# Running the second half of a projection chunk's blocks one piece of weights behind the first half

## The chip, the cores and the metric

The kernel runs on one core of one Trainium2 chip. Its time is the device time of one execution in microseconds, and the number compared is the median over several executions. Engines are named as in the profile: PE is TensorE, with PEld for its weight loads, DVE is VectorE, ACT is ScalarE, POOL is GpSimd, and SP is the queue that issues the DMAs.

## What is computed

The reference is a decoder trunk of two layers over 256 tokens of width 2048, all in float32. Cut to what matters here, one layer is:

```python
h = rms_norm(x, pre_g)
p = split_columns(h @ w_in + b_in)        # 2048 x 6992: 14 groups of up to 512 columns here
o_sb  = stick_breaking_attention(...)     # four head groups, each reads its columns of p
o_nsa = native_sparse_attention(...)      # compressed keys and values by two small networks
o_fox = forgetting_attention(...)
o_mla = latent_attention(...)             # low-rank: w_uq and w_ukv on 512 columns of p
mix = concatenate([o_g * silu(gate_g) for g in (sb, nsa, fox, mla)])
x = x + rms_norm(mix @ w_out, post_g)
```

Most of the work is `h @ w_in`, with `mix @ w_out` next. The change touches the order of the first.

## The kernel before, in words

**Operands.** The normalised input stands transposed in eight tiles `hcat`, one for each pair of K tiles of 128 rows. Each holds a high part of all 256 tokens and beside it the low part (what rounding to the high part left). The weights come as a stream of *pieces* (class `Stream`, L170): a piece is 256 rows by up to 512 columns, loaded into a `raw` tile by DMA, and split by two instructions for each of its two halves: ACT copies `raw` into the high part `whi` (`hi()`, L211), then DVE subtracts that from `raw` into the low part `wlo` (`lo()`, L226). A product is the sum of high by high, high by low and low by high.

**Chunks.** A *chunk* is one group of columns against all of K, so eight pieces. `chunk()` (L573) works on two to four *blocks*, each with an accumulator of one PSUM bank. A T block (`mm_t()`, L640) gives 128 output columns as partitions: for each half of a piece one matmul of 512 columns (high weights against both parts of `hcat`, L648) and one of 256 (low weights, L649). Its two sums are added on evacuation (`evac_t()`, L664: ACT copies one half, DVE adds, POOL multiplies by the norm factor). A K block (`mm_k()`, L652) has 128 tokens as partitions: six matmuls for a piece (L660), and DVE evacuates it (`k_out()`, L632). `t_group()` (L672) is a chunk of four T blocks, `k_group()` (L721) one of two K blocks, and `nsa_kv()` (L1056) has two T blocks and one with both token halves. The accumulators come from a pool of four banks that are taken in turn, `mm`.

In `chunk()` the loop over pieces is the outer one, and every piece goes through all the blocks before the next:

```python
for ks in range(NK // 2):
    hi, lo = self.ws.get()
    for i, (b, o) in enumerate(zip(blocks, acc)):
        ...                       # the block's matmuls with this piece
        if last:
            evac(i, o)
    self.ws.free()
```

`first_chunk()` (L594) and `out_proj()` (L1412) have loops of their own.

**Order.** The order on every engine is written out by the program itself; engines wait for each other by semaphores. A planner keeps an estimated clock of PE and of the queues on DVE, ACT and POOL. After every few matmuls `pump()` (L287) moves PE's clock on and lets one step of one waiting task (attention heads, gates, rotations, the compression networks) write its instructions when the estimates say that its inputs are there, so that those matmuls and transposes stand between the projection's. Then `Stream.tick()` (L239) may write one split. `get()` (L252) writes whatever of the next piece isn't split yet. Splits run ahead of use up to a limit that counts from the last *freed* piece: eight `whi`/`wlo` tiles, of which `spare` (two) stay back. `raw` loads follow the splits, up to four pieces (L207), and other loads are put between them on SP (`later()`, L358).

**The places spoken of below.** In each layer `nsa_q()` (L1155), a chunk of two K blocks, is followed by `mla_up()` (L939). That takes one piece of `mla_w_ukv` and three of `mla_w_uq` (384 columns a half), and its matmuls are on L955: the products for v (evacuated by ACT to `mv`), for kn (DVE copies to `kn`), for qr and for qn. Each matmul for qr reads both halves of a piece (`heads()`, L968). Then come the mla gate, a K chunk of 336 columns, `nsa_kv()`, the nsa gate, the sb queries, keys and values, and so on. `qq` is the rotated nsa query that PE transposes on L1176; `pc` (L1250) is the softmax of the compressed branch; `w` are the weights of the compression networks (L1115), loaded in four parts for keys and four for values.

Of the kernel before, what the change touches and what calls it, by code (L numbers as in the profile page):

```python
# [19 lines left out]
S = 256  # L20
# [3 lines left out]
NK = D // P  # L24
# [243 lines left out]
class Kernel:  # L268
# [304 lines left out]
    def chunk(self, blocks, evac):  # L573

        acc = self.accs(len(blocks))
        for ks in range(NK // 2):
            last = ks == NK // 2 - 1
            hi, lo = self.ws.get()  # L580
            for i, (b, o) in enumerate(zip(blocks, acc)):
                if b[0] == "T":
                    self.mm_t(o, hi, lo, b[1], ks)
                elif b[0] == "K":
                    self.mm_k(o[:, :b[3]], self.h_at(ks, b[1]), hi, lo, b[2], b[3], ks == 0, last)
                else:
                    for t in range(2):
                        self.mm_k(o[:, t * S:(t + 1) * S], self.h_at(ks, t), hi, lo, b[1], S, ks == 0 and t == 0, last)
                if last:
                    self.now()  # L590
                    evac(i, o)
            self.ws.free()

    def first_chunk(self, l, cols):  # L594

# [996 lines left out]
```

## Time and profile before

| | |
|---|---|
| median of 3 runs | 949.1 us (948.77 to 949.96) |
| the profiled execution | 947.95 us |
| its span, first to last instruction | 946.2 us |
| PE, PEld busy | 924.5, 782.6 us |
| DVE, ACT, POOL busy | 604.9, 521.8, 119.0 us |
| matmuls of the T blocks (L648, L649) | 396.2 + 304.0 us busy |
| matmuls of the K blocks (L660 on `hcat`) | 229.9 + 138.9 us busy |
| TensorE clock granted, mean | 0.998 |

A line of a timeline reads: start, duration, engine, source line, operation, out<-in, shapes, count, and in brackets the idle time before it with what ended it. A line of the waits reads: who waited for whom, us in total, times, longest. Matmuls overlap in the pipeline, so two rows' starts tell the pace, and their durations do not add up. Most instructions of DVE, ACT and POOL have the line of one recording helper (L127), so they are told apart by their tiles.

### The profile page before, as it was taken

The numbers are of one execution on the slowest core, as the hardware profiler recorded it, in microseconds if no ns is written. First come the engines' busy times: TensorE is split into PE (matmuls) and PEld (weight loads), VectorE is DVE, ScalarE is ACT, GpSimd is POOL, SyncE is SP. The second block draws the span as 40 slices with busy tenths as digits, with TensorE's granted clock in tenths as the row PEclk, the third lists the DMA queues.
The fourth block names the chain that finished last, engine by engine and source line by source line (L and its number), as shares of the span: only waits on it lengthen the run. The fifth ranks groups of instructions, "written<-read, shape, count | busy, mean of one in ns | idle before, by whom it ended". The sixth has DMA issues, their size and how long they took to land.

```text
span 946.2 us, 14525 instructions
## 1 busy us (share of the span) xinstructions
PE 924.5 (98%) x5186; PEld 782.6 (83%) x5186; DVE 604.9 (64%) x1324; ACT 521.8 (55%) x1176; POOL 119.0 (13%) x190
## 2 busy tenths in 40 slices
PE   7999999999999999999999999999999999999996
PEld 6888988877888888888878999878778888888885
DVE  6786777646666656754486867676457675557552
ACT  6745554544567554744476565456355775447540
POOL 0231011111011210100002210212100221001000
PEclk9999999999999999999999999999999999999999
DMA  7857656784354754579368575478644455646852
GB/s 269 271 180 192 188 180 184 238 252 120 115 155 132 225 189 127 162 265 307 96 200 269 161 191 182 137 212 260 200 122 136 154 152 184 209 134 220 263 185 89
DMA packets 116912, 177.65 MB, mean 188 GB/s; under 512 B 15860, under 2 KB 39400, under 8 KB 116840
## 3 DMA queue, kind: packets, MB, share of 16 engines
q1 hardware_dynamic: 116840, 176.73, 60.5%
q8 instruction: 40, 0.66, 0.3%
q14 instruction: 32, 0.26, 0.1%
HBM read 172.51 MB, written 4.19 MB: 187 GB/s over the span
## 4 chain that ended last, share of the span: by engine, by line
PE 88%; DMA 6%; DVE 3%; ACT 2%; POOL 1%; issue 1%; SPq 0%; POOLq 0%; DVEq 0%; ACTq 0%
PE mm L660 39%; PE mm L648 24%; PE mm L649 12%; PE sp L761 3%; DMA raw<-w_in 2%; PE mm L955 2%; PE op L805 1%; DMA w<-nsa_cmp_w_k 1%; DMA w<-nsa_cmp_w_v 1%; PE sp L793 1%; PE op L1115 1%; PE op L806 1%; ACT whi L127 1%; PE sp L496 1%; DVE wlo L127 1%
## 5 line engine op out<-in xcount | busy, mean ns | idle before, releaser
L127 DVE TENSOR_TENSOR wlo<-raw,whi 128x512 fp32r<-128x512 f32 (+2 forms) x592 | 389.3, 702 | 68.3 <-ACT whi L127 67.3
L648 PE MATMUL mm<-hcat,whi 128*128 128x512 f32 x1088 | 396.2, 405 | 2.3 <-DVE cmpT L127 1.2
L127 ACT ACTIVATE whi<-raw 128x512 fp32r<-128x512 f32 (+2 forms) x592 | 331.1, 613 | 117.1 <-DMA raw<-w_in 69.7
L649 PE MATMUL mm<-hcat,wlo 128*128 128x256 f32 x1088 | 304.0, 279 | 0.0
L648 PEld LDWEIGHTS mm<-hcat,whi 128*128 128x128 f32 x1088 | 204.5, 188 | 52.6 <-issue 4.5
L660 PE MATMUL mm<-whi,hcat 128*128 128x512 f32 (+2 forms) x768 | 229.9, 371 | 0.8 <-DVE tgrp L127 0.8
L649 PEld LDWEIGHTS mm<-hcat,wlo 128*128 128x128 f32 x1088 | 205.4, 189 | 0.2
L660 PEld LDWEIGHTS mm<-whi,hcat 128*128 128x128 f32 x768 | 139.1, 189 | 22.1 <-DVE tgrp L127 2.0
L660 PE MATMUL mm<-wlo,hcat 128*128 128x512 f32 (+2 forms) x384 | 138.9, 362 | 1.3 <-DVE wlo L127 1.3
L660 PE MATMUL mm<-whi,mxh 128*128 128x512 f32 x256 | 99.8, 390 | 0.0
L660 PE MATMUL mm<-whi,mxl 128*128 128x512 f32 x256 | 99.6, 389 | 0.0
L660 PE MATMUL mm<-wlo,mxh 128*128 128x512 f32 x256 | 99.6, 389 | 0.0
L127 POOL TENSOR_TENSOR tgrp<-tgrp,rr 128x256 f32<-128x256 f32 x64 | 58.3, 933 | 255.2 <-DVE tgrp L127 255.0
L660 PEld LDWEIGHTS mm<-wlo,hcat 128*128 128x128 f32 x384 | 72.6, 189 | 11.6 <-DVE wlo L127 2.9
L660 PEld LDWEIGHTS mm<-whi,mxl 128*128 128x128 f32 x256 | 48.0, 188 | 10.0
L660 PEld LDWEIGHTS mm<-whi,mxh 128*128 128x128 f32 x256 | 48.1, 188 | 10.0
L660 PEld LDWEIGHTS mm<-wlo,mxh 128*128 128x128 f32 x256 | 48.1, 188 | 9.9
L127 ACT ACTIVATE z<-z,nm 128x128 f32<-128x128 f32 x64 | 28.5, 447 | 48.2 <-DVE nm L127 47.1
L127 DVE TENSOR_TENSOR tgrp<-mm,tpart 128x256 f32<-128x256 f32 x64 | 26.1, 420 | 45.0 <-ACT tpart L127 44.8
L127 DVE CUSTOM_DVE_ANT_0 z<-sp,cst 128x128 f32<-128x128 f32 x64 | 20.3, 355 | 40.5 <-PE sp L761 40.4
L127 ACT ACTIVATE tpart<-mm 128x256 f32<-128x256 f32 x68 | 24.6, 380 | 37.8 <-PE mm L649 37.6
L127 DVE TENSOR_TENSOR y<-mm,bct 128x512 f32<-128x512 f32 x16 | 11.1, 692 | 51.3 <-ACT junk L127 51.3
(223 smaller groups left out, 755.1 us busy)
## 6 DMA issues: line engine op xcount, KB each, us to landing
raw<-w_in SPq DMA_DIRECT2D x207, 512.0 KB, 4.5
raw<-w_out SPq DMA_DIRECT2D x64, 512.0 KB, 5.0
x<-x SPq DMA_DIRECT2D x24, 256.0 KB, 6.3
raw<-w_in SPq DMA_DIRECT2D x16, 268.0 KB, 3.6
w<-nsa_cmp_w_k SPq DMA_DIRECT2D x8, 512.0 KB
w<-nsa_cmp_w_v SPq DMA_DIRECT2D x8, 512.0 KB, 6.2
raw<-mla_w_uq SPq DMA_DIRECT2D x6, 384.0 KB, 5.0
bct<-b_in SPq DMA_DIRECT2D x8, 256.0 KB, 5.3
```

The lines of the kernel that those rows point to most:

```text
L127: return f(out, *args, **kw)
L496: nc.tensor.transpose(ps[:, k * P:(k + 1) * P], x[:, k * P:(k + 1) * P], self.ident)
L648: nc.tensor.matmul(o, wh, h, start=(ks + kk == 0), stop=False, skip_group_check=True)
L649: nc.tensor.matmul(o[:, :S], wl, h[:, :S], start=False, stop=last, skip_group_check=True)
L660: nc.tensor.matmul(o, x, w, start=(first and kk == 0 and i == 0), stop=(last and kk == 1 and i == 2), skip_group_check=True)
L761: nc.tensor.matmul(sp[:, a:a + s1], q[:, q0:q0 + P], k[:, :s1], start=(i == 0 and a == 0), stop=(i == n - 1), skip_group_check=True)
L793: nc.tensor.transpose(sp[:, i * P:(i + 1) * P], z[:, i * P:(i + 1) * P], self.ident)
L805: nc.tensor.matmul(o, v0, pt[:, :256], start=start, stop=False, skip_group_check=True)
L806: nc.tensor.matmul(o[:, 128:256], v1, pt[:, 256:384], start=False, stop=stop, skip_group_check=True)
L955: nc.tensor.matmul(o, a, b, start=(i == 0 and o is first[0]), stop=(i == len(mms) - 1), skip_group_check=True)
L1115: nc.tensor.matmul(hp[g:g + 32, :P], blks[i][:, q * 8 + j, :], ws[q][:, j * P:(j + 1) * P], start=(q == 0 and j < 4), stop=(q == 3 and j > ...
```

## The change

Within `chunk()` the blocks are divided into an early half (`len(blocks) // 2`) and a late half. Step by step the early blocks take piece `step`, and then the late blocks take piece `step - 1`. A piece is freed after the late blocks have used it, so two pieces are held while the early blocks run. The chunk has nine steps instead of eight: in the first only the early blocks run, in the last only the late ones. The early blocks' accumulators are evacuated at the end of their last piece, when the late blocks still have two pieces to go. No matmul, split or load is added or removed. Since the planner writes side work and splits between the matmuls, their places move as well.

```diff
         acc = self.accs(len(blocks))
-        for ks in range(NK // 2):
-            last = ks == NK // 2 - 1
-            hi, lo = self.ws.get()
-            for i, (b, o) in enumerate(zip(blocks, acc)):
...
-                if last:
-                    self.now()
-                    evac(i, o)
-            self.ws.free()
+        n = NK // 2
+        held = {}
+
+        def run(i, ks):
+            b, o = blocks[i], acc[i]
+            hi, lo = held[ks]
+            last = ks == n - 1
...
+            if last:
+                self.now()
+                evac(i, o)
+
+        early = len(blocks) // 2
+        for step in range(n + 1):
+            if step < n:
+                held[step] = self.ws.get()
+                for i in range(early):
+                    run(i, step)
+            if step:
+                for i in range(early, len(blocks)):
+                    run(i, step - 1)
+                self.ws.free()
```

The lines left out hold the three kinds of block, which are the same on both sides. In the changed kernel everything below `chunk()` stands 14 lines lower: L648, L649, L660 and L955 there are L662, L663, L674 and L969.

More of the change, by code (lines that the diff above doesn't have):

```diff
@@ L577, in chunk @@
         acc = self.accs(len(blocks))
-        for ks in range(NK // 2):
-            last = ks == NK // 2 - 1
-            hi, lo = self.ws.get()
-            for i, (b, o) in enumerate(zip(blocks, acc)):
[L582 to L588, printed above, removed]
-                if last:
-                    self.now()
-                    evac(i, o)
-            self.ws.free()
+        n = NK // 2
[4 more added lines that the diff above has]
+            last = ks == n - 1
+            if b[0] == "T":
+                self.mm_t(o, hi, lo, b[1], ks)
+            elif b[0] == "K":
+                self.mm_k(o[:, :b[3]], self.h_at(ks, b[1]), hi, lo, b[2], b[3], ks == 0, last)
+            else:
+                for t in range(2):
+                    self.mm_k(o[:, t * S:(t + 1) * S], self.h_at(ks, t), hi, lo, b[1], S, ks == 0 and t == 0, last)
+            if last:
[11 more added lines that the diff above has]
+                self.ws.free()
     def first_chunk(self, l, cols):
```

## The prediction

> **What bounds the kernel now.** I read the page first, then the list of waits, then the timelines of the places that the list names.
>
> ```profile
> PE 924.5 (98%) x5186; PEld 782.6 (83%) x5186; DVE 604.9 (64%) x1324; ACT 521.8 (55%) x1176; POOL 119.0 (13%) x190
> PEclk9999999999999999999999999999999999999999
> PE 88%; DMA 6%; DVE 3%; ACT 2%; POOL 1%; issue 1%; SPq 0%; POOLq 0%; DVEq 0%; ACTq 0%
> ```
>
> TensorE is busy for 924.5 of 946.2 us at a clock that is full in every slice, and 88% of the chain that ended last is PE. The matmuls themselves are the same before and after, so the change can only act on what is left: the time in which PE waits, some 22 us with the start and the end. PE's own waits, longest first, from the list of waits filtered to PE:
>
> ```profile
> PE sp L496 <- DMA x<-x: 3.1, 2, 2.0
> PE op L460 <- DMA grow<-pre_norm_g: 2.5, 1, 2.5
> PE mm L660 <- DVE wlo L127: 1.3, 1, 1.3
> PE op L1115 <- DMA w<-nsa_cmp_w_v: 1.3, 2, 0.9
> PE mm L648 <- DVE cmpT L127: 1.2, 2, 0.7
> PE mm L648 <- DVE tgrp L127: 1.1, 2, 0.6
> PE op L1115 <- DMA w<-nsa_cmp_w_k: 1.1, 1, 1.1
> PE sp L1250 <- POOL pc L127: 0.9, 2, 0.5
> PE mm L660 <- DVE tgrp L127: 0.8, 1, 0.8
> PE sp L1176 <- DVE qq L127: 0.5, 1, 0.5
> ```
>
> Only the three rows on cmpT and tgrp belong to chunk() itself: 1.2 + 1.1 + 0.8 = 3.1 us in five waits. They are the first matmuls of a chunk that wait until the accumulator of the chunk before has been evacuated. One of them, from the chunk of the sb queries to that of the sb keys in layer 0 (timeline of all engines, start and duration in us):
>
> ```profile
> 189.61 0.28 PE L649 MATMUL mm<-hcat,wlo 128*128 128x256 f32 x1
> 189.94 0.91 ACT L127 ACTIVATE tpart<-mm 128x256 f32<-128x256 f32 x3
> 189.97 0.28 PE L649 MATMUL mm<-hcat,wlo 128*128 128x256 f32 x1
> 190.33 0.76 DVE L127 TENSOR_TENSOR tgrp<-mm,tpart 128x256 f32<-128x256 f32 x2 [1.45 <-ACT tpart L127]
> 190.81 0.50 PE L648 MATMUL mm<-hcat,whi 128*128 128x512 f32 x1 [0.57 <-DVE tgrp L127]
> 191.15 0.28 PE L649 MATMUL mm<-hcat,wlo 128*128 128x256 f32 x1
> 191.27 0.40 PE L648 MATMUL mm<-hcat,whi 128*128 128x512 f32 x1
> ```
>
> In steady flow an L649 start is followed by the next L648 start after 0.12 us (191.15 to 191.27); here it takes 0.84 us (189.97 to 190.81). So a wait costs 0.72 us where the list says 0.57: the pipeline runs empty as well. Five such waits cost 3.1 + 5 x 0.15 = 3.9 us.
>
> **The change part by part.** *The end of a chunk.* On TensorE, at this same boundary, the first matmul of each block in the rows before (hcat_274 is the last pair of K tiles; mm_1976 to mm_1979 are the four accumulators of the queries, mm_2292 and mm_2293 the first two of the keys, which take the banks of the queries' first two):
>
> ```order
> L648 MATMUL mm_1977<-hcat_274,whi_2074 128x512
> ...
> L648 MATMUL mm_1978<-hcat_274,whi_2074 128x512
> ...
> L648 MATMUL mm_1979<-hcat_274,whi_2074 128x512
> ...
> L648 MATMUL mm_2292<-hcat_135,whi_2124 128x512
> ...
> L648 MATMUL mm_2293<-hcat_135,whi_2124 128x512
> ```
>
> The same place now, where mm_2010 to mm_2013 are the queries' and mm_2292 and on the keys':
>
> ```order
> L662 MATMUL mm_2011<-hcat_274,whi_2104 128x512
> ...
> L662 MATMUL mm_2012<-hcat_273,whi_2093 128x512
> ...
> L662 MATMUL mm_2013<-hcat_273,whi_2093 128x512
> ...
> L662 MATMUL mm_2012<-hcat_274,whi_2104 128x512
> ...
> L662 MATMUL mm_2013<-hcat_274,whi_2104 128x512
> ...
> L662 MATMUL mm_2292<-hcat_135,whi_2144 128x512
> ...
> L662 MATMUL mm_2293<-hcat_135,whi_2144 128x512
> ```
>
> Between an accumulator's last matmul and the first one that overwrites its bank three blocks stood, and now five stand. A T block is two pairs of L648 and L649, and a pair takes 0.35 us (189.61 to 189.97 in the rows above), so a block takes 0.7 and the cover grows from 2.1 to 3.5 us. At the other boundaries the order shows as many blocks or more. In the quoted wait the cover fell short by 0.57 us; the longest of the five, 0.8 us, is less than the 1.4 us gained. I count all five waits as gone: **-3.9 us**. What is late next there is nothing: the banks of the late half are first written after both early halves of the next chunk, again five blocks. Of the steps that move, the early half's evacuation (in the rows above ACT's copy of 0.3 us, VectorE's add of 0.4, then GpSimd's multiply) now runs four blocks ahead of the late half's; it issues no DMA, and the two engines get it in two parts instead of one. 0 us.
>
> *The weights.* From its second piece on, a chunk now wants each piece half a piece (1.4 us) earlier, and holds one piece longer, so that the split runs half a piece to one piece less far ahead. PE waits for wlo once, 1.3 us, and that is in first_chunk(), which the change leaves alone. The nearest place in a chunk is the start of the mla gate in layer 0:
>
> ```profile
> 64.42 2.43 DVE L127 TENSOR_TENSOR wlo<-raw,whi 128x512 fp32r<-128x512 f32 x3
> 67.85 0.40 PE L648 MATMUL mm<-hcat,whi 128*128 128x512 f32 x1
> ```
>
> The first piece and the first half of the second are ready at 66.8 and PE needs the second some 2.8 us after 67.85, now 1.4. Nothing is late; if this cover were gone, each piece would cost what it lacks. 0 us.
>
> *mla_up, the price that I see.* nsa_q()'s chunk comes just ahead of mla_up(). Since the stream frees later, the split of the last mla_w_uq piece slips on VectorE behind the evacuation of kn. Before, in layer 1 (kgrp: the two evacuations of the nsa queries; wlo of 384 columns: halves of the mla_w_uq pieces):
>
> ```order
> L127 SCALAR_TENSOR_TENSOR kgrp<-mm,rc,bct 128x512
> L127 TENSOR_TENSOR wlo<-raw,whi 128x384 x2
> L127 SCALAR_TENSOR_TENSOR kgrp<-mm,rc,bct 128x512
> L127 TENSOR_TENSOR qq<-kgrp,cst 128x512
> L127 TENSOR_TENSOR qq<-qq,ropet 128x512
> L127 COPY kn<-mm 128x512 x2
> L127 TENSOR_TENSOR wlo<-raw,whi 128x512 x2
> ```
>
> Now:
>
> ```order
> L127 SCALAR_TENSOR_TENSOR kgrp<-mm,rc,bct 128x512
> L127 TENSOR_TENSOR wlo<-raw,whi 128x384 x2
> L127 SCALAR_TENSOR_TENSOR kgrp<-mm,rc,bct 128x512
> L127 TENSOR_TENSOR qq<-kgrp,cst 128x512
> L127 TENSOR_TENSOR qq<-qq,ropet 128x512
> L127 COPY kn<-mm 128x512 x2
> L127 TENSOR_TENSOR wlo<-raw,whi 128x384
> L127 TENSOR_TENSOR qq<-kgrp,cst 128x512
> ```
>
> All six halves stood ahead of the two copies of kn; the sixth now stands behind them. The eighth matmul of mla_up's product for qr reads both halves of the third piece at once (heads(), L968), so it must wait for that sixth half. Layer 1, timelines of VectorE and TensorE:
>
> ```profile
> 525.43 0.74 DVE L127 SCALAR_TENSOR_TENSOR kgrp<-mm,rc,bct 128x512 f32<-128x512 f32 x1
> 526.10 0.67 DVE L127 TENSOR_TENSOR qq<-kgrp,cst 128x512 f32<-128x512 f32 x1
> 526.88 1.06 DVE L127 TENSOR_TENSOR qq<-qq,ropet 128x512 f32<-128x512 f32 x1
> 527.86 1.28 DVE L127 COPY kn<-mm 128x512 f32<-128x512 f32 x2
> ...
> 527.24 0.28 PE L955 MATMUL mm<-wlo,cTh 128*128 128x256 f32 x1
> ```
>
> Up to the copies VectorE's order is unchanged, so they end at 529.1 as before. One half takes 0.55 us (row below), which gives 529.65; PE wanted it at 527.24. That is **+2.4 us** in layer 1, in a place where PE does not wait today. In layer 0:
>
> ```profile
> 58.24 0.55 DVE L127 TENSOR_TENSOR wlo<-raw,whi 128x384 fp32r<-128x384 f32 x1
> 60.69 1.22 DVE L127 TENSOR_TENSOR qq<-qq,ropet 128x512 f32<-128x512 f32 x1 [0.64 <-POOL ropet L127]
> 61.83 1.28 DVE L127 COPY kn<-mm 128x512 f32<-128x512 f32 x2
> 61.08 0.28 PE L955 MATMUL mm<-wlo,cTh 128*128 128x256 f32 x1
> 61.20 0.28 PE L955 MATMUL mm<-whi,cTl 128*128 128x256 f32 x1
> 61.96 0.66 PE L1176 MATMUL sp<-ident,qq 128*128 128x128 f32 x4 [0.48 <-DVE qq L127]
> ```
>
> There the mla transposes ahead of it stand three matmuls of 0.23 us earlier, so I move VectorE's chain forward by 0.7 us: the copies end at 63.1 - 0.7 = 62.4, the half at 63.0, and PE, which wants it at 61.08, waits 1.9 us. But today the transposes of qq wait right after (61.96 instead of 61.32, 0.6 us), and that wait is swallowed. Net **+1.2 us**. Ends: 0.6 and 1.9.
>
> A rule of the Trainium skill touches the half's 0.55 us: GPSIMD Engine Reference, § 1. Specifications, says that GpSimd shares its SBUF interfaces with VectorE and that they contend when VectorE reads two SBUF inputs, as this subtraction does. The trace agrees. Two halves alone, and two under GpSimd's rope:
>
> ```profile
> 516.52 1.02 DVE L127 TENSOR_TENSOR wlo<-raw,whi 128x384 fp32r<-128x384 f32 x2
> 523.95 1.57 DVE L127 TENSOR_TENSOR wlo<-raw,whi 128x384 fp32r<-128x384 f32 x2
> 524.11 4.42 POOL L127 TENSOR_TENSOR ropet<-kgrp,cst 128x256 f32<-128x256 f32 x4 [8.15 <-DVE kgrp L127]
> ```
>
> The rope ends at 528.5, before the late half would start at 529.1, so I keep 0.55; under a rope it would be 0.8 (1.57 / 2) and both layers together 0.5 us dearer.
>
> *The side work.* The planner's tasks of the nsa branch move ahead of the blocks, by about 30 projection matmuls (5 us) in layer 0 and 10 to 20 in layer 1, with those that feed them. Two kinds run close. The softmax of the compressed branch (pc) makes PE wait in layer 1 (0.9 us above); in layer 0 it does not, but there the boundary wait of 0.8 us that I take away came just ahead of it. I take +0.4 us, the middle of 0 and 0.9. The compression weights' DMAs are waited for today in three rows' worth, 1.3 + 1.1 = 2.4 us. Their uses and issues shift by different amounts; from none of it to twice, -2.4 to +2.4, and I take +0.3, near the middle because places of both signs are among the sixteen.
>
> **Sum**: -3.9 + 2.4 + 1.2 + 0.4 + 0.3 = +0.4 us. The profiled execution took 947.95 us (span 946.2, 1.75 around it), so 948.35 for that one; against the median of the runs, 949.1, I forecast 949.5 us. About 0.2%, 1.9 us, is what a measurement of this kernel can tell from no change.
>
> **The rivals.**
> *The price is not paid (faster).* VectorE reaches the sixth half sooner than I think, because earlier evacuations shorten its queue ahead of mla_up. For it: ACT and DVE are busy 55% and 64% only. Against it: the quoted chain hangs on GpSimd's rope and the evacuation of the second half, which the change does not move forward in layer 1. With no wait the sum is -3.9 + 0.7 = -3.2, 945.9 us; with half, 947.7. Chance 0.22.
>
> *The compression weights (slower).* Place: the loads of nsa_kv()'s compress(), which stand in SP's queue behind weight loads that wait for VectorE. 40 projection matmuls lay between the third load of layer 1 and its use in the order in which the program is written out, now 30; for the second value load of layer 0 42, now 34.
>
> ```profile
> SPq L159 <- DVE wlo L127: 612.8, 251, 13.7
> DMA to landing us min/median/max: 5.3/6.2/7.7
> ```
>
> A matmul of a T block takes 0.17 us on average, so 30 of them are 5.2 us, under the shortest landing of 5.3: from there on each matmul lost is paid. Price 10 x 0.17 + 8 x 0.17 = 3.1 us in place of 0.3: 952.3 us. Against it: six other loads gain 2 to 12 matmuls and four lose only 2 to 4. Chance 0.18.
>
> *The change does not do what it says (slower).* Evacuations still reach VectorE too late, because they queue behind splits that are now issued closer. Then -3.9 falls away: 953.4 us. Against it: the longest shortfall is 0.8 us and 1.4 us are added. Chance 0.06.
>
> *The clock (slower).* If a wait in mla_up makes the clock step down, the matmuls behind it run slower. No row here shows it: PE waits up to 2.0 us (L496) and every slice of PEclk reads 9. If as much work as each wait lasts, 1.9 and 2.4 us, then took double its time, that would be +4.3 us on top: 953.8. Chance 0.04. The Trainium skill, TensorE: Matmul & The Clock Gate, § What's actually happening, puts the step to half the clock at an idle window of about 3.4 us; by that rule a wait of 2.4 us changes nothing, and the trace agrees as far as its 2.0 us go.
>
> **How the numbers follow.** My forecast of no change worth measuring has 0.50 (947.2 to 951.0, the sizes of pc, the DMAs and layer 0 within their ends). Faster 0.22, slower 0.18 + 0.06 + 0.04 = 0.28, same 0.50. The range takes in half of the price unpaid (947.7) and the weights' case (952.3). It leaves out the far end of the faster case, where nothing of the price is paid (945.9, some 0.08), and the last two slower cases (0.10): 946.2 to 952.6.
>
> **What would show it.** Right: no PE row on tgrp or cmpT left among the waits; a new row of some 4 us on PE L969 waiting for DVE wlo, twice, near 61 and 525 us; the row on qq gone. Wrong: tgrp rows still there (first step); no wlo wait in mla_up, or one under 1 us (the price); rows on the nsa_cmp weights of over 5 us (side work); a slice of PEclk under 9.

## The result, and the profile after

The changed kernel takes 960.0 us (median of 4 runs, 957.68 to 961.95) against 948.93 us (median of 4, 948.17 to 949.96) before, a ratio of 1.0115 (95% interval 1.0093 to 1.0138). It is slower by some 11 us. I had forecast 949.5 us, with 946.2 to 952.6 as the range and 0.28 on slower. The profiled execution took 957.68 us, 9.7 us more than the one of before (947.95).

The busy time of PE has hardly moved (924.5 us before), so nearly all that was lost is waiting; one stretch of slower clock comes in below. Two rows of the page, then PE's own waits, where the last two numbers are the count and the longest one:

```profile
PE 924.9 (97%) x5186; PEld 785.4 (82%) x5186; DVE 602.9 (63%) x1324; ACT 521.5 (55%) x1176; POOL 122.7 (13%) x190
PEclk9999999999999999999999999999999999999998
```

```profile
PE op L1129 <- DMA w<-nsa_cmp_w_v: 5.3, 3, 2.5
PE mm L969 <- DVE wlo L127: 4.6, 2, 2.4
...
PE mm L662 <- DVE tgrp L127: 2.6, 2, 1.4
...
PE sp L1264 <- POOL pc L127: 1.7, 4, 0.5
PE op L1129 <- DMA w<-nsa_cmp_w_k: 1.5, 1, 1.5
PE mm L674 <- DVE wlo L127: 1.3, 1, 1.3
```

The new row on L969 is the price that I had forecast for mla_up. The rows on cmpT and qq and one of the tgrp rows are gone as forecast, but a tgrp row is left: 2.6 us in two waits of 1.4 and 1.2, at the two places where 0.6 each stood before. The rows on the compression weights have grown from 2.4 to 6.8 us. That the last PEclk slice reads 8 is the tail behind PE's last matmul.

**mla_up.** VectorE and TensorE in layer 1. The half-split of mla_w_uq stands behind the two copies of kn, and the matmul that reads it starts when it ends:

```profile
531.27 1.05 DVE L127 TENSOR_TENSOR qq<-qq,ropet 128x512 f32<-128x512 f32 x1
532.25 1.27 DVE L127 COPY kn<-mm 128x512 f32<-128x512 f32 x2
533.44 0.54 DVE L127 TENSOR_TENSOR wlo<-raw,whi 128x384 fp32r<-128x384 f32 x1
...
531.51 0.28 PE L969 MATMUL mm<-whi,cTh 128*128 128x256 f32 x1
534.04 0.56 PE L969 MATMUL mm<-wlo,cTh 128*128 128x256 f32 x1 [2.25 <-DVE wlo L127]
534.40 0.42 PE L969 MATMUL mm<-whi,cTl 128*128 128x256 f32 x1
```

From 531.51 to 534.04 are 2.53 us where the pace is 0.12: 2.4 us lost, as forecast. The second thing to see is in the durations: the first matmul behind the wait takes 0.56 us and not 0.28. Layer 0:

```profile
61.96 1.27 DVE L127 COPY kn<-mm 128x512 f32<-128x512 f32 x2
63.16 0.54 DVE L127 TENSOR_TENSOR wlo<-raw,whi 128x384 fp32r<-128x384 f32 x1
...
63.75 0.39 PE L969 MATMUL mm<-wlo,cTh 128*128 128x256 f32 x1 [2.37 <-DVE wlo L127]
```

**The boundary that I had counted as gone.** The end of the sb queries in layer 0, rows of all engines from one timeline. The queries' four evacuations are the four tpart rows on ACT:

```profile
188.21 0.39 ACT L127 ACTIVATE tpart<-mm 128x256 f32<-128x256 f32 x1 [2.83 <-PE mm L663]
...
189.13 1.12 POOL L127 TENSOR_TENSOR tgrp<-tgrp,rr 128x256 f32<-128x256 f32 x1 [7.21 <-DVE tgrp L127]
...
190.28 0.51 ACT L127 ACTIVATE tgrp<-tgrp,cols 128x256 f32<-128x256 f32 x1 [1.69 <-POOL tgrp L127]
...
190.70 0.37 ACT L127 ACTIVATE tpart<-mm 128x256 f32<-128x256 f32 x1
...
192.75 0.51 ACT L127 ACTIVATE tgrp<-tgrp,cols 128x256 f32<-128x256 f32 x1 [1.69 <-POOL tgrp L127]
...
194.21 0.36 ACT L127 ACTIVATE tpart<-mm 128x256 f32<-128x256 f32 x1
...
196.25 0.51 ACT L127 ACTIVATE tgrp<-tgrp,cols 128x256 f32<-128x256 f32 x1 [1.68 <-POOL tgrp L127]
196.66 0.36 ACT L127 ACTIVATE tpart<-mm 128x256 f32<-128x256 f32 x1
...
197.06 0.42 DVE L127 TENSOR_TENSOR tgrp<-mm,tpart 128x256 f32<-128x256 f32 x1 [1.44 <-ACT tpart L127]
197.40 4.87 DVE L127 TENSOR_TENSOR wlo<-raw,whi 128x512 fp32r<-128x512 f32 x7
...
197.54 0.51 PE L662 MATMUL mm<-hcat,whi 128*128 128x512 f32 x1 [1.42 <-DVE tgrp L127]
...
198.16 0.37 SPq L159 DMA_DIRECT2D raw<-w_in  x1
...
198.88 0.37 SPq L159 DMA_DIRECT2D w<-nsa_cmp_w_v  x1
...
204.26 0.65 PE L1129 MATMUL op<-w,blk 128*32 128x128 f32 x16 [2.51 <-DMA w<-nsa_cmp_w_v]
```

Between each two evacuations stands the bias instruction of the first (ACT, tgrp from tgrp and cols), and it sits there for 1.7 us until GpSimd has multiplied. So ACT's copy, VectorE's add, GpSimd's multiply and ACT's bias run one after the other, and the next evacuation begins only then: 2.5 us from 188.21 to 190.70, and 8.4 us from the first copy to the fourth (between the second and the third two of the splits' copies, 1.13 us, stand on ACT as well). PE waits for the fourth at 197.54. VectorE's seven splits stand behind that add as well, the load of raw on SP's queue waits for a split, and the load of w stands behind that load: it goes out at 198.88, and PE waits for it at 204.26. That is one chain from a bias instruction on ACT to a DMA; whether it holds is what the second experiment asks.

### The profile page after: what moved, and what is told of

The parts are those of the page before. It is cut to its first block, busy times and chain, and to the rows that moved or that the text cites. A ratio compares the mean times of both kernels' runs of the same rounds, so it can differ in the third digit from the quotient of the medians.

```text
span 956.0 us, 14510 instructions
## 1 busy us (share of the span) xinstructions
PE 924.9 (97%) x5186; PEld 785.4 (82%) x5186; DVE 602.9 (63%) x1324; ACT 521.5 (55%) x1176; POOL 122.7 (13%) x190
## 4 chain that ended last, share of the span: by engine, by line
PE 89%; DMA 3%; DVE 3%; ACT 2%; POOL 1%; issue 1%; SPq 0%; POOLq 0%; DVEq 0%; ACTq 0%
PE mm L674 41%; PE mm L662 24%; PE mm L663 12%; PE sp L775 3%; PE op L819 1%; PE mm L969 1%; DMA w<-nsa_cmp_w_v 1%; PE sp L807 1%; DMA raw<-w_in 1%; ACT whi L127 1%; DMA w<-nsa_cmp_w_k 1%; PE op L820 1%; DVE wlo L127 1%; POOL tgrp L127 1%; PE sp L496 1%
## 5 line engine op out<-in xcount | busy, mean ns | idle before, releaser
L127 DVE TENSOR_TENSOR wlo<-raw,whi 128x512 fp32r<-128x512 f32 (+2 forms) x592 | 385.3, 695 | 52.5 <-ACT whi L127 51.8
L662 PE MATMUL mm<-hcat,whi 128*128 128x512 f32 x1088 | 396.0, 404 | 2.6 <-DVE tgrp L127 2.6
L663 PE MATMUL mm<-hcat,wlo 128*128 128x256 f32 x1088 | 304.1, 279 | 0.0
L662 PEld LDWEIGHTS mm<-hcat,whi 128*128 128x128 f32 x1088 | 204.6, 188 | 51.3 <-issue 4.3
L674 PE MATMUL mm<-whi,hcat 128*128 128x512 f32 (+2 forms) x768 | 228.5, 370 | 0.0
L663 PEld LDWEIGHTS mm<-hcat,wlo 128*128 128x128 f32 x1088 | 205.3, 189 | 0.3
L674 PEld LDWEIGHTS mm<-whi,hcat 128*128 128x128 f32 x768 | 139.1, 189 | 20.6 <-issue 1.0
L674 PE MATMUL mm<-wlo,hcat 128*128 128x512 f32 (+2 forms) x384 | 138.9, 362 | 1.3 <-DVE wlo L127 1.3
L674 PE MATMUL mm<-whi,mxh 128*128 128x512 f32 x256 | 99.8, 390 | 0.0
L674 PE MATMUL mm<-whi,mxl 128*128 128x512 f32 x256 | 99.6, 389 | 0.0
L674 PE MATMUL mm<-wlo,mxh 128*128 128x512 f32 x256 | 99.6, 389 | 0.0
L127 POOL TENSOR_TENSOR tgrp<-tgrp,rr 128x256 f32<-128x256 f32 x64 | 62.1, 980 | 276.4 <-DVE tgrp L127 276.2
L674 PEld LDWEIGHTS mm<-wlo,hcat 128*128 128x128 f32 x384 | 72.6, 189 | 11.4 <-DVE wlo L127 2.5
L674 PEld LDWEIGHTS mm<-whi,mxh 128*128 128x128 f32 x256 | 48.0, 188 | 10.0
L674 PEld LDWEIGHTS mm<-whi,mxl 128*128 128x128 f32 x256 | 48.0, 188 | 10.0
L674 PEld LDWEIGHTS mm<-wlo,mxh 128*128 128x128 f32 x256 | 48.1, 188 | 9.8
```

The lines of the kernel that those rows point to most:

```text
L127: return f(out, *args, **kw)
L662: nc.tensor.matmul(o, wh, h, start=(ks + kk == 0), stop=False, skip_group_check=True)
L663: nc.tensor.matmul(o[:, :S], wl, h[:, :S], start=False, stop=last, skip_group_check=True)
L674: nc.tensor.matmul(o, x, w, start=(first and kk == 0 and i == 0), stop=(last and kk == 1 and i == 2), skip_group_check=True)
```

## The experiments

Theory A came from these rows and has three prices. (1) The hold: a piece is freed later, the splits run less far ahead, and the sixth half of mla_w_uq slips behind the copies of kn. (2) The bias instructions between the evacuations, with the tgrp and most of the w waits behind them. (3) The clock, which steps down behind some of the long waits. The rivals are given with each run. All medians and waits stand first, so that the runs can be compared. The ratio is to the kernel before, run beside them on the same chip (949.5 us beside e1 to e4, 949.6 beside e5 to e8, 949.7 beside e9 to e12); the waits are sums from the list of PE's waits of the profiled execution, and the last column counts the stretches of 3.41 us at half clock behind a wait in that execution.

| | median us | ratio to before | wlo in mla_up | tgrp, cmpT | w | half clock |
|---|---|---|---|---|---|---|
| before | 948.9 | | 0 | 3.1 | 2.4 | 0 |
| after | 960.0 | 1.0115 (1.0093, 1.0138) | 4.6 | 2.6 | 6.8 | 1 |
| e1 after, longer look-ahead | 953.5 | 1.0044 (1.0032, 1.0056) | 0 | 0.7 | 10.0 | 1 |
| e2 after, bias behind | 951.0 | 1.0022 (1.0011, 1.0033) | 4.6 | 0 | 2.8 | 3 |
| e3 before, late free only | 957.8 | 1.0090 (1.0073, 1.0106) | 5.6 | 4.7 | 1.4 | 2 |
| e4 after, e1 and e2 | 945.8 | 0.9959 (0.9947, 0.9971) | 0 | 0 | 4.5 | 0 |
| e5 after, PE kept busy | 959.9 | 1.0112 (1.0096, 1.0128) | 0.5 | 1.6 | 8.0 | 2 |
| e6 before, e1 and e2 | 945.8 | 0.9957 (0.9945, 0.9970) | 0 | 0.4 | 4.3 | 0 |
| e7 before, bias behind | 947.0 | 0.9971 (0.9960, 0.9981) | 0 | 2.1 | 3.7 | 0 |
| e8 e4 and a third tile | 942.6 | 0.9927 (0.9914, 0.9941) | 0 | 0 | 2.9 | 0 |
| e9 after, nsa queries as before | 956.4 | 1.0066 (1.0054, 1.0078) | 0 | 3.2 | 6.3 | 3 |
| e10 before, lag in nsa queries | 954.2 | 1.0052 (1.0040, 1.0064) | 4.5 | 3.0 | 1.9 | 0 |
| e11 after, third tile | 952.9 | 1.0030 (1.0021, 1.0039) | 4.7 | 0 | 3.6 | 2 |
| e12 e6 and a third tile | 946.7 | 0.9967 (0.9954, 0.9980) | 0 | 0.4 | 1.6 | 1 |

**e1, a longer look-ahead.** On the changed kernel, in the stream and in `first_chunk()`:

```diff
-        self.spare = 2
+        self.spare = 1
```

> The changed kernel with one number changed: the splits may run one piece further ahead (one tile kept back instead of two), which makes up for the piece that a chunk now holds longer. In the written order all six halves of mla_w_uq stand ahead of the copies of kn again; ACT's order at the sb queries is as in the changed kernel. Theory A (three separate prices: the late half-split at mla_up, ACT's bias instructions between the evacuations of the sb queries, and clock steps that follow TensorE idle times of over 2 us): the two waits for wlo in mla_up go (2.5 + 2.4 us, of which 0.6 comes back as the wait for qq), and with them about half of the clock loss; the waits for tgrp (1.6 + 1.4) and w stay. 952.5 to 956 us against 960.0 for the changed kernel. Rival B (the shorter look-ahead is behind the late w as well, since loads of w stand behind loads of raw): 948 to 951.

953.5 us, 6.5 us less than the changed kernel and inside theory A's 952.5 to 956. The two mla_up waits are gone and the w waits are not, so the shorter look-ahead isn't what makes w late:

```profile
PE op L1129 <- DMA w<-nsa_cmp_w_v: 8.5, 4, 3.0
...
PE op L1129 <- DMA w<-nsa_cmp_w_k: 1.5, 1, 1.5
...
PE mm L662 <- DVE tgrp L127: 0.7, 1, 0.7
```

The tgrp waits shrank too, which I had not expected. The evacuations are as slow as in the changed kernel (at the same place ACT's copies start at 187.14, 189.63, 193.13 and 195.58), but PE now waits 0.9 us for w at 190.79, between them; as I read it, that wait takes up time in which it would have waited for tgrp. A wait that leaves the list has not always lost its cause.

**e2, the bias behind the evacuations.** On the changed kernel:

```diff
             if gate is None:
-                self.spawn(bias)
+                biases.append(bias)
...
+        biases = []
         self.chunk([("T", h * P) for h in range(4)], evac)
+        for bias in biases:
+            self.spawn(bias)
```

> The changed kernel, with the four bias instructions of a T chunk (ACT, tgrp<-tgrp,cols) written only after all four evacuations of the chunk. Theory A: in the changed kernel each bias stands on ACT between two evacuations and waits there for GpSimd, so that evacuations follow each other every 2.4 us instead of 0.4 to 0.7; that holds up the fourth bank (waits for tgrp, 1.6 + 1.4 us), VectorE's splits behind it, and through them the loads of raw and w on SP's queue (waits for the value weights w, 2.7 and 2.5 us). All of these go or shrink to below 1 us each: 6 us, and 953 to 955 us; the two waits in mla_up stay at 2.4 to 2.5 us. Rival B: only the waits for tgrp go, 3 us, w comes as late as before: 957 us. Rival C: ACT's order costs nothing, 960 us.

951.0 us, 9.0 us less than the changed kernel and 2 us below theory A's range. ACT at the end of the sb queries, layer 0:

```profile
193.24 0.38 ACT L127 ACTIVATE tpart<-mm 128x256 f32<-128x256 f32 x1 [3.95 <-PE mm L663]
193.95 0.38 ACT L127 ACTIVATE tpart<-mm 128x256 f32<-128x256 f32 x1 [0.33 <-PE mm L663]
...
196.07 0.38 ACT L127 ACTIVATE tpart<-mm 128x256 f32<-128x256 f32 x1 [0.70 <-PE mm L663]
196.77 0.39 ACT L127 ACTIVATE tpart<-mm 128x256 f32<-128x256 f32 x1 [0.32 <-PE mm L663]
...
198.09 1.70 ACT L127 ACTIVATE tgrp<-tgrp,cols 128x256 f32<-128x256 f32 x4
```

Each copy now waits for PE and not for GpSimd: 3.5 us for the four where it was 8.4. Among PE's waits:

```profile
PE mm L972 <- DVE wlo L127: 4.6, 2, 2.4
...
PE op L1132 <- DMA w<-nsa_cmp_w_k: 2.1, 1, 2.1
...
PE op L1132 <- DMA w<-nsa_cmp_w_v: 0.7, 2, 0.4
```

No row on tgrp or cmpT is left, the value weights went from 5.3 to 0.7 us, and mla_up has not moved. So the chain from the bias to the value weights' DMA holds, and rivals B and C fall. The key weights' wait grew by 0.6 us. How the 9.0 us divide stays open: the profiled execution, 955.06 us, is the slowest of the twelve, with three stretches at half clock, and it is only 2.6 us below the changed kernel's. By the list its waits are 6.6 us shorter, and two more stretches cost 3.4. The other executions' mean clocks are 0.994 to 0.998, three of the changed kernel's four 0.990 to 0.992, so part of the 9.0 is clock.

**e3, the late freeing alone.** The changed kernel with `early = len(blocks)`: all blocks take the same piece, as before the change, and a piece is freed one piece late, as with the change.

> The order of the matmuls in a chunk as before the change; only the freeing of a piece is one piece late, as the change makes it. In the written order the fifth and the sixth half of mla_w_uq stand behind the copies of kn. Theory A: the price at mla_up comes from the hold alone, so PE waits for wlo in both layers, 2.4 to 3.1 us each (two halves instead of one), with clock steps behind these waits in part of the executions: 953 to 958 us against 949 for the kernel before. The boundary waits stay as before (0.6 to 0.9 us each). Rival: the new order is what costs, and the hold is free: 949 us.

957.8 us (1.0090): the hold alone, without any new order, costs 8.3 us. The fifth and sixth half are both late in mla_up; and the boundary waits, which I had expected to stay, more than doubled for tgrp (1.9 before):

```profile
PE mm L969 <- DVE wlo L127: 5.6, 2, 2.9
PE mm L662 <- DVE tgrp L127: 4.0, 4, 1.4
```

No bias makes them at the sb queries of layer 0: there ACT's four copies stand in a row, and VectorE's add for the fourth stands behind a rotation of the compressed keys (kc) that waits for GpSimd; PE then waits 1.1 us for that add.

```profile
197.19 0.29 DVE L127 TENSOR_TENSOR kc<-kc,ropet 128x128 f32<-128x128 f32 x1 [1.19 <-POOL ropet L127]
197.40 0.42 DVE L127 TENSOR_TENSOR tgrp<-mm,tpart 128x256 f32<-128x256 f32 x1
```

So theory A's three prices are not separate: the hold by itself also moves side work in front of an evacuation. What made the other three waits was not followed.

**e4, both edits of e1 and e2 on the changed kernel.**

> Both edits on the changed kernel: one piece more of look-ahead, and the bias instructions behind the evacuations. Theory A: both prices and the clock steps go, and the gain at the chunk boundaries (3.9 us) is left, with a small price for pc: 945 to 948 us, below the kernel before. Rival (the order of the half-lagged chunk has a price of its own that the waits don't show, 2 us or more): 950 us or more.

945.8 us: 14.2 less than the changed kernel, where e1 and e2 alone gave 6.5 + 9.0 = 15.5, and 0.4% below the kernel before. Of the waits that the change brought, those for w are left in part (4.5 us in all, 3.3 for the value weights), and the 1.7 us for pc.

**e5, PE kept busy during the mla_up waits.** On the changed kernel, ahead of the eighth matmul of the product for qr (`spin` is the bank of the next product, which overwrites it):

```diff
+                if spin is not None and i == 7:
+                    for _ in range(18):
+                        nc.tensor.matmul(spin, ch[:, 0, :P], wq[0][0][:, 0, :S], start=True, stop=True,
+                                         skip_group_check=True)
                 nc.tensor.matmul(o, a, b, start=(i == 0 and o is first[0]), stop=(i == len(mms) - 1),
```

> The changed kernel with 18 extra matmuls of 128x256 (some 2.2 us at the 0.12 us that this shape takes in mla_up) put just ahead of the matmul that waits for the late half-split, in both layers; their results are overwritten. They fill the idle time and do not shorten the wait: the matmul starts when VectorE has the split, as before. Theory A (a TensorE idle of over 2 us is followed in part of the executions by 3.4 us at half clock, 1.7 us lost): no clock step behind mla_up in the profile, a mean clock of 0.994 or more in most runs against 0.990 to 0.995, and 956.5 to 958.5 us against 960.0. Rival B (the clock steps have nothing to do with the wait, or cost nothing): 960 us. Rival C (the extra matmuls don't fit into the wait): 961 us or more.

959.9 us, no change: theory A's time was wrong here, and rival B's was right. Theory A's mechanism is in line with the profile: the idle row in mla_up falls to 0.5 us for both layers, and no stretch of half clock follows either (without the extra matmuls that holds for e10 as well, so one execution proves little). But this execution has two stretches elsewhere, one of them behind a wait for w of 4.0 us. Its four executions have mean clocks of 0.994, 0.992, 0.992 and 0.994, those of the changed kernel 0.995, 0.990, 0.992 and 0.990. So the run doesn't settle how much of the median the clock makes.

**e6, the kernel before with the edits of e1 and e2.** No lag.

> The kernel before the change with both edits of the fastest run so far (one piece more of look-ahead, the bias instructions behind the evacuations), so without the half-lagged order. Theory A (the lag itself is worth the boundary waits, 3.9 us): those waits stay, 948 to 950 us, against 945.8 with the lag. Rival B (the gain came from the two edits, the lag is worth nothing): 944.5 to 946.5 us.

945.8 us, the same as e4: rival B, and theory A was wrong. With these two edits the lag brings nothing, since the old order then has hardly a boundary wait left (0.4 us on cmpT). It costs nothing either: without the edits the changed kernel takes 11 us more than the kernel before, with them in both there is no difference left. So the whole loss hangs on what the two edits touch. The kernel before gains 3.8 us by them too, so not all of e4's 14.2 us was the change's.

**e7, the kernel before with the bias behind alone.**

> The kernel before the change with the bias instructions behind the evacuations alone. Before, only one of the four bias instructions stands between evacuations (the first), so theory A expects little: two of the five boundary waits (0.85 and 0.65 us, at the sb queries) shrink, 948 to 949.5 us against 949.5. Rival B (the bias instructions are what costs at the boundaries in both kernels, lag or not): all five shrink, 946 us.

947.0 us, between the two forecasts. The tgrp waits at the sb queries went (1.1 us), 1.3 us on cmpT and 0.8 us on tgrp stayed, and the waits for w grew by 1.3, so the list accounts for none of the 2.7 us. (The 0.85 and 0.65 us that the expectation puts at the sb queries are nearer to the two cmpT waits with their restarts; at the sb queries the list has 0.57 twice.) The profiled executions can't show it either: this kernel's, 947.92 us, is among its slowest, that of the kernel before, 947.95, is below all four behind its median, and both spans are 946.2 us. Where the 2.7 us lie stays open.

**e8, a third tile for the compression weights**, on e4:

```diff
-                ws = [self.slot("w1") for _ in range(2)]
+                ws = [self.slot("w1") for _ in range(3)]
...
                 w1_load(1)
+                w1_load(2)
...
-                    if q + 2 < 4:
-                        w1_load(q + 2)
+                    if q + 3 < 4:
+                        w1_load(q + 3)
```

(The bound inside `w1_load()` moves by one too.)

> The fastest version so far (the changed kernel with one piece more of look-ahead and the bias instructions behind), and the compression weights loaded three parts ahead instead of two. Theory A (what is left of the waits for w, 3.3 and 1.2 us, is late issue on SP's queue): most of it goes, 942 to 944 us. Rival B (the transfer or the place of the loads behind raw loads sets it, not the number of tiles): 945 to 947 us.

942.6 us, as theory A had it, 3.2 us below e4 and the fastest of all: 0.9927 (0.9914 to 0.9941) of the kernel before.

**e9, the nsa queries as before the change.** The changed kernel; `k_group()` hands a flag to `chunk()`, and in this one chunk all blocks take the same piece and it is freed at once.

> The changed kernel, but the chunk of the nsa queries (just ahead of mla_up) has its order and its freeing from before the change; all other chunks lag. Theory A (the waits in mla_up come from that one chunk): both waits for wlo go (2.5 + 2.4 us), the wait for qq (0.6) is back, and the clock steps behind them go as well; the waits for tgrp and w stay. 953 to 956 us against 960.0. Rival B (the mla_w_uq splits are late because of the chunks ahead or the whole stream): 958 us or more.

956.4 us, 3.6 less, 0.4 above theory A's range. Both mla_up waits are gone with one chunk, so rival B falls. This execution has three stretches at half clock, all behind waits for w.

**e10, the lag in the nsa queries alone**, on the kernel before.

> The kernel before the change with the lag in the chunk of the nsa queries alone. Theory A: two waits of 2.3 to 2.5 us for wlo in mla_up and no other new wait; PE is idle there for over 2 us, so in part of the executions a clock step of 1.7 us follows. 949.5 + 4.3 + 0 to 3.4: 953.5 to 957 us. Rival B (side work later in the layer absorbs part of the delay, since some of its waits have an end that doesn't move): 950 to 953 us.

954.2 us, 4.5 more than the kernel before (949.7): the two waits in mla_up are 4.5 us by the list, the qq wait of 0.5 is gone, and no other new row is over 0.4 us. This is the price that the prediction put at +2.4 and +1.2, measured by itself; rival B falls.

**e11, the third tile alone**, on the changed kernel.

> The changed kernel with the compression weights loaded three parts ahead instead of two, and nothing else changed. Theory A (the waits for w, 7.5 us in the changed kernel, are late issues on SP behind splits that wait for the evacuations): most of them go, with the clock steps behind them; the waits in mla_up and for tgrp stay. 952 to 955 us. Rival B (the tgrp waits take what the w waits give back): 957 us or more.

952.9 us, 7.1 less, as theory A had it. The w waits halved, from 6.8 to 3.6 us by the list (the expectation's 7.5 counts 0.15 for each restart). The tgrp waits went as well, against the expectation, although ACT's four copies still take as long:

```profile
187.10 0.38 ACT L127 ACTIVATE tpart<-mm 128x256 f32<-128x256 f32 x1 [0.57 <-PE mm L663]
...
195.54 0.36 ACT L127 ACTIVATE tpart<-mm 128x256 f32<-128x256 f32 x1
```

That is 8.4 us, as in the changed kernel. But PE now has two groups of w matmuls between the first copy and the fourth, with 0.6 us of waiting for w, where the changed kernel had one group; as I read it, they fill PE's time until the copies are done.

**e12, the third tile on e6**, no lag.

> The kernel before the change with the three edits of the fastest version (look-ahead, bias behind, third weight tile), without the lag. Theory A (once the three prices are gone, the lag is worth nothing that can be measured, as between 945.79 with it and 945.77 without): 942 to 943.5 us, as 942.6 with the lag. Rival B (the waits for w had covered a gain of the lag): 944.5 to 946 us without it.

946.7 us, 4 us above e8, where theory A wanted no difference, and 0.7 above rival B's range. Between e4 and e6 the lag was worth nothing, here 4 us: the third tile brings 3.2 us with the lag (e8) and nothing without it (e6 has 945.8), although the w waits fall from 4.3 to 1.6. In the two profiles (spans 945.2 and 940.5) 1.7 us is a stretch of half clock that only e12 has, and the waits for qq and cmpT that only e12 has are 0.5 and 0.4 us. What the lag is worth by itself in a kernel without its prices stays open.

## Why the prediction was wrong, step by step

**The end of a chunk, -3.9: wrong, and the step that failed.** The prediction said that the evacuations move and that "it issues no DMA, and the two engines get it in two parts instead of one. 0 us." The cover did grow, and three of the five waits went, by the list 1.2 us on cmpT and 0.8 on tgrp. At the end of the sb queries, one in each layer, the evacuations grew more than the cover: 1.1 us in two waits became 2.6. In all 3.1 us in five became 2.6 in two; with 0.15 for each restart 3.9 became 2.9, so -1.0 in place of -3.9. Nor is an evacuation without effect on DMAs: VectorE's splits stand behind its adds, and SP's loads wait for the splits. The cause was to be seen in the trace of before, ACT at the same place:

```profile
187.45 0.38 ACT L127 ACTIVATE tpart<-mm 128x256 f32<-128x256 f32 x1 [2.23 <-PE mm L649]
189.52 0.51 ACT L127 ACTIVATE tgrp<-tgrp,cols 128x256 f32<-128x256 f32 x1 [1.69 <-POOL tgrp L127]
189.94 0.91 ACT L127 ACTIVATE tpart<-mm 128x256 f32<-128x256 f32 x3
```

The prediction quoted the third row, and the first two stand just above it: the first bias already sat for 1.7 us in front of three evacuations. Before, one bias stands between evacuations; with the lag three do, and the fourth comes behind the last copy. From the code I would say why: the planner writes no ordinary task while it believes ACT or VectorE to be over 1 us behind, evacuations in a row put them behind, and the lag sets four blocks between the second and the third; this was not tried by itself. The rival "evacuations still reach VectorE too late", which I gave 0.06, had the place and the direction, but another mechanism (splits issued closer, not a bias on ACT) and too high a price. I argued against it with the size of the shortfall, 0.8 us against 1.4 gained, without following what stands between the evacuations on ACT.

**The compression weights, +0.3: mis-sized, the largest error.** They rose from 2.4 to 6.8 us, +4.4, beyond the end of +2.4 that I gave. I moved each load by the number of matmuls between it and its use. What counts is what stands ahead of it on SP's queue: raw loads that wait for splits, which waited for the evacuations. e2 shows it for the value weights, down from 5.3 to 0.7 us; the key weights (1.5 us) did not gain by it. The rival of the compression weights had the sign, at 0.18, and the wrong place: it named the third key load of layer 1 and the second value load of layer 0, and the waits stand at the third value load of both layers.

**mla_up, +2.4 in layer 1: right**, 2.4 us at the place named and for the reason named (e1, e9 and e10). **Layer 0, +1.2: too small.** The wait is 2.5 us from start to start, less the 0.6 for qq that is swallowed, +1.9, the end that I gave. The step that failed is that I moved VectorE's chain forward by 0.7 us: the copies of kn start at 61.96 and before at 61.83.

**pc, +0.4: right in kind.** 0.9 us in two waits became 1.7 in four, +0.8 by the list, inside the ends of 0 and 0.9.

**The clock, not in the sum.** I gave it 0.04 and said that no row showed it. The rows that I leaned on say nothing either way: the waits of 2.0 us on L496, and of 2.5 on L460, stand in the first 7 us, and the record of the granted clock starts at 10.1 us, so PEclk reads 9 there whatever the clock was. Two matmuls of the same form, before:

```profile
8.79 0.80 PE L660 MATMUL mm<-wlo,hcat 128*128 128x512 f32 x1
10.20 0.40 PE L660 MATMUL mm<-wlo,hcat 128*128 128x512 f32 x1
```

So behind these waits TensorE runs at half its later pace; whether because of them or from the start, this trace can't tell, and it was no support for a clock that stays. Later it does step down. The windows view of the changed kernel, with PE's busy time first and PEclk ahead of the last two columns:

```profile
527.27:530.68 3.41, 3.41 (x22) 3.02 (x22) 3.41 (x7) 2.89 (x6) 2.05 (x3) 1.00 0.20 23
530.68:534.10 3.42, 1.17 (x11) 0.96 (x9) 3.32 (x6) 0.00 (x0) 2.23 (x2) 1.00 0.36 130
534.10:537.51 3.41, 3.41 (x16) 3.41 (x17) 3.31 (x6) 1.63 (x3) 0.00 (x0) 0.50 0.56 154
537.51:540.92 3.41, 3.41 (x31) 3.41 (x30) 0.98 (x2) 2.21 (x5) 1.73 (x4) 1.00 0.89 261
```

Behind the mla_up wait PE has half clock for 3.41 us, which loses 1.7 us of work. The sign that I named for it, a slice of PEclk under 9, could not show it: a slice is 23.9 us long, and 1.7 lost still reads 9. As for the sizes, the profiled execution has one such stretch; the execution of 961.95 us has a mean clock of 0.990 against its 0.995, 4.8 us less work over 956 us, and is 4.3 us longer.

**The sum.** -1.0 + 2.4 + 1.9 + 0.8 + 4.4 + 1.7 = +10.2 us, where the two profiled executions differ by 9.7; 0.5 us is left over. Forecast were +0.4. 4.1 us of the error are the weights, 2.9 the boundaries, 1.7 the clock, 0.7 layer 0 and 0.4 pc.

## What to carry to other kernels

When an order moves on one engine, write out what then stands between two dependent instructions on each of the engines behind it; here one instruction of 0.5 us, which waits for GpSimd, set the pace of four evacuations and through VectorE and SP's queue the arrival of a DMA. A buffer that is held one step longer takes that step from the look-ahead of everything that shares its pool, and the price shows at the next place where splits were just in time. Judge a repair by undoing the cause and not by the row that disappears: a wait can be covered by another (e1, e11), and the wait that remains may get longer.

## What the runs showed of the hardware

The clock steps on a fixed grid. Eight of the fourteen profiles have stretches at half clock between their start and their tail. Within an execution these lie on one grid of 3.41 us and last 3.41 us, once twice that (e9). The clock of a window goes with what PE did in the one before. Leaving out each execution's start and tail, all eleven windows at full clock with at most 1.46 us of PE busy were followed by half clock, and none with 1.95 or more was; of the thirteen between 1.5 and 1.95 three were. A window at half clock was followed by full clock where PE was busy for 3.1 us or more of it, and by a second one at half clock in the one case with 2.8. Two windows of e5, PE's busy time first:

```profile
673.17:676.58 3.41, 1.28 (x20) 0.99 (x21) 0.00 (x0) 0.02 (x1) 0.00 (x0) 1.00 1.06 371
676.58:679.99 3.41, 3.41 (x13) 2.92 (x12) 0.00 (x0) 0.00 (x0) 0.00 (x0) 0.50 0.95 281
```

So a wait of 2.2 to 2.4 us is dear or cheap by where it falls on the grid: waits of that length in mla_up were followed by half clock in both layers of e2, in layer 1 alone of the changed kernel, and in neither of e10. The wait of 1.3 us at the start of layer 1, which every profile has, was followed by it twice, in e5 and e12, where other short waits lay in the same window. The Trainium skill, TensorE: Matmul & The Clock Gate, § What's actually happening, describes a free-running window of 3413 ns, and the grid here agrees. It puts the step down at an idle window; the window of the mla_up wait in layer 1 of the changed kernel was a third busy, 1.17 us of 3.41, and the measurement decides.
